# A hybrid encoder layer on one core: half of the mixer's output projection in seven products instead of eight

## The chip, the core and the metric

The kernel runs on one core of a Trainium2 chip. The metric is the device time of one execution in microseconds. The engines named below are TensorE (PE in the rows; PEld is its weight load), VectorE (DVE), ScalarE (ACT), GpSimd (POOL), which here mainly issues transfers, and SyncE (SP), whose queue issues nearly all loads. Each engine works through its own list of instructions in a fixed order, and semaphores tie them together.

## The reference, cut to what matters

```python
mixed = jnp.concatenate(
    [rms_norm(attn, g_attn_out[i]), rms_norm(rec, g_rec_out[i])], axis=-1) @ w_out[i]
h = h + rms_norm(mixed, g_mix_post[i])
fn = rms_norm(h, g_ffn_pre[i])
ff = (jax.nn.silu(fn @ w_ffn_gate[i]) * (fn @ w_ffn_up[i])) @ w_ffn_down[i]
```

There are 256 rows and 2048 columns. The output projection is the product with w_out (2048 by 2048, fp32). In front of it stand attention and a recurrent block, behind it the FFN and a per-layer embedding.

## The kernel before

**How the work is tiled.** Every large product is cut into column chunks of 512 and pairs of row blocks (two blocks of 128 rows of the weights). One *tile* is one such pair, 128 x 1024 values, 512 KB. Each tile is loaded into a raw buffer (`wr`, four of them), ScalarE casts it to fp32r (`wh`, line 661), VectorE takes the remainder of that cast (`wl`, line 677), and TensorE multiplies: for each of two row blocks and two halves of the 256 activations three products of 128 x 512, high by high, low by high, high by low (lines 715 to 717). That is 12 matmuls a tile. Four pairs of `wh` and `wl` exist, so a tile can be cast only when the tile four places ahead of it has been multiplied; a raw buffer is free again after `wl`.

**Seven products.** In the FFN, two neighbouring column chunks of one pair of row blocks are taken together as a 2 x 2 by 2 x 2 block product, in Winograd's form: seven products instead of eight, 21 matmuls instead of 24. Sums of weight blocks (lines 605 to 611, and one by a transfer that adds, line 630) and of activation blocks (`sums_of`, lines 827 to 834, and a split) are made first. Such a *unit* has four parts: `four_products` (two tiles, 12 matmuls, into all four accumulators), `made_of_four` (differences between the accumulators), `two_products` (6 matmuls) and `one_product` (3 matmuls).

**The output projection.** Chunks 0, 1 and 2 take turns, tile by tile, through eight pairs of row blocks (attention's four, `A_KS`, then the recurrent block's four, `R_KS`); chunk 3 follows alone. `sub_post` then squares each chunk and multiplies it by a gain into `mg` (lines 1558 and 1540); `next_norm` makes the root from the squares and adds `mg` times it to the residual `h` (line 1598). Two tiles of the embedding's product (`embedding`) stand between chunk 3 and the transposes of `h` (line 334), with which the FFN begins. `open_p2` opens the second stage's memory when chunk 0 ends, and `load_p2` loads the gain, `pw` and `h` from there.

**What sets the order.** A planner (`Plan`) keeps a clock for each engine while the program is written and puts into each engine's list whatever it expects to be able to start first. So a change in one place can reorder the side work on VectorE and ScalarE anywhere later. On the chip nothing is reordered.

Of the kernel before, what the change touches and what calls it, by code (L numbers as in the profile page):

```python
# [16 lines left out]
P = 128  # L17
# [10 lines left out]
N = 512  # L28
# [12 lines left out]
DOWN_KS = (0, 2, 4, 6)  # L41
PLE_KS = (0, 2)
BEGIN = (6, 7)
OUT = (3, 6, 7, 1)
# [11 lines left out]
    ),  # L56
    (lambda c: (("w_ple_gate", c), ("w_ple_gate", c + 1)), (2,), PLE_KS),
]

# [184 lines left out]
def layer(ctx: ExitStack, tc: tile.TileContext, a: dict, out: bass.AP):  # L244
# [160 lines left out]
    class Chunk:  # L405
        def __init__(self, post, before=None, late=0.0, slot="acc"):
            self.post, self.before, self.late, self.slot = post, before, late, slot
            self.accs, self.made = None, None
            self.ready, self.free = Event(), Event()
# [30 lines left out]
    class Group:  # L440
# [23 lines left out]
        def two(self, j):  # L464
            i = len(tiles)
            tiles.append(None)
            self.twos[j] = i
            lower[self.own[j] + 1] = -1
            segs.append((two_products, self, j, i))
# [70 lines left out]
    def load_stream():  # L540
        for i, tl in enumerate(tiles):
# [3 lines left out]
            w, k, n0 = tl  # L545
            if min(fours) <= i < i_ple:
                if i in lower:
                    yield (ev_spilled, ev_half_spilled, ev_unmerged)[(0, 0, 1, 2, 2)[lower[i]]]
                yield dma(ISSUE, take=raw_kind(i))
                t = lower_tile(lower[i]) if i in lower else raw_tile(i)  # L550
                nc.sync.dma_start(t, a[w][n0 // N, k // 2])
                plan.now += COST["landing"]
                if i in ev_load:
                    loaded[i] = t
                    done(ev_load[i])
                else:
                    raws[i] = t
                    done(ev_raw[i, 2])
                continue
            if i in ev_load:  # L560
# [26 lines left out]
    def sum_stream():  # L587

        for i in sorted(fours):
            at_end = i in ends_with  # L590
            for e in () if at_end else fours[i][4].values():
                yield e
# [5 lines left out]
            if at_end:  # L598
                yield ev_big
            elif n or j == 3:  # L600
                yield ev_half_spilled
            Q, R = loaded.pop(i), loaded.pop(i + 1)
            yield dve(N, take=None if at_end else f"T{n}")
            both = last_blocks(2)[:, 2 * j : 2 * j + 2, :] if at_end else blocks()[:, b0 : b + 1 : b - b0, :]
            nc.vector.tensor_tensor(out=both[:, 0, :], in0=Q[:, 0, :], in1=Q[:, 1, :], op=ALU.add)
            yield dve(N, take=None if at_end else f"t{j}")
            nc.vector.tensor_tensor(out=both[:, 1, :], in0=both[:, 0, :], in1=R[:, 1, :], op=ALU.add)  # L607
# [7 lines left out]

    ends_with, ends_in = {}, {}

    def last_blocks(i):
# [15 lines left out]
    def last_sum(i):  # L634
        late, last, j, js, _, _ = fours[i]
        b = OUT[j]
        there, at_end = Event(), i in ends_with
        yield from added(last_blocks(2)[:, 2 * j + 1, :] if at_end else blocks()[:, b, :], late[:, 0, :], there)
        yield there
        if j == js[-1]:  # L640
            raws[last] = last_blocks(2)[:, 1:4:2, :] if at_end else blocks()[:, slice(3, 7, 3) if not js[0] else slice(1, 8, 6) if js[1:] else slice(7, 8), :]
            done(ev_raw[last, 2])
# [21 lines left out]
    def ffn_fours():  # L664
        return {i: f for i, f in fours.items() if i not in ends_with}

# [72 lines left out]
    def four_products(group, j, i):  # L739
# [3 lines left out]
        first, last = j == 0, j == len(group.sevens) - 1  # L743
        if first:
            C1.open()
            C2.open()
        plan.main(0, ev_lo[i, 2], group.lhs.ev[kx], ev_s, C1.ready, C2.ready)
        s = group.lhs.sums[kx]
        product(C2.accs[0], s["S1"], i, 0, first, last)
        product(C2.accs[1], s["S2"], i, 1, first, last)  # L750
        spent(i)
        plan.main(0, ev_lo[i + 1, 2])
        product(C1.accs[0], block(group.lhs, kx, 0), i + 1, 0, first, last)
        product(C1.accs[1], s["S7"], i + 1, 1, first, last)
        spent(i + 1)
        if last:
            plan.add(made_of_four(group), plan.clk["pe"] + plan.SEM, -SOON)
            plan.run()

    def made_of_four(group):  # L760
# [49 lines left out]
    def sums_of(lhs, kx, hi, lo):  # L810
# [6 lines left out]
        yield lhs.ev[kx + 1]  # L817
        kind = "mid" if lhs is hP else "T4"
        for j in range(2):
            h, l = lhs.at[kx + j]  # L820
            yield dve(S, take=None if j else kind)
            if not j and lhs is hP:
                at_ = mid_tile()
# [541 lines left out]
    def attend(g):  # L1365
# [32 lines left out]
        yield ev_in  # L1398
        at_hi, at_lo = hT_pair("attn")
        mixT.blocks(at_hi, at_lo, 2, H - 2, 2)  # L1400
        for bs in ((2, 6), (4,)):
            plan.add(attn_norm(bs, ra, at_hi, at_lo), plan.now)

    at0 = tuple(at.tile([P, 2, S], F32R, name=f"at0_{n}") for n in ("hi", "lo"))
# [51 lines left out]
    def open_p2():  # L1456
# [4 lines left out]
        t2["pool"] = rs  # L1461
        t2["h"], t2["mg"] = Halves(rs, "h"), Halves(rs, "mg")
        t2["ple"] = rs.tile([P, NT, D], F32, name="ple")
        t2["third"] = rs.tile([P, 2, N], F32, name="third")
        plan.add(load_p2(), plan.clk["pe"])

    pT = [Act(2)] * 2
# [14 lines left out]
    def load_p2():  # L1482
# [15 lines left out]
        pT[0].blocks(hi, lo, 0, 2)  # L1498
        pT[0].pair(0)

    ev_sums_back = Event()

    class Sub:
# [10 lines left out]
        def chunk(self, c, ch, add=False):  # L1514
# [9 lines left out]
            for t in range(NT):  # L1524
                src = ch.accs[t]
                if add:
                    yield dve(N)
# [200 lines left out]
    def after_mix():  # L1728
# [3 lines left out]
    A_KS = [(k, k) for k in range(0, 8, 2)]  # L1732
    OPEN = 3
    ch = [
        Chunk(sub_post(mix, c, after=after_mix), None if c else open_p2,
              slot="sm" if c == 2 else "acc")
        for c in range(4)
    ]
# [399 lines left out]
    n = 0  # L2138
    for i in range(min(fours), max(f[1] for f in ffn_fours().values())):
# [4 lines left out]
    for i in range(min(fours), max(f[1] for f in fours.values() if f[4] is hF.ev_sums)):  # L2144
        if i % (W_BUFS + MORE_W) < MORE_W:
# [4 lines left out]
    for i, (_, last, _, js, _, two) in fours.items():  # L2150
        ev_load[i], ev_load[i + 1] = Event(), Event()
        if i in ends_with:
            gives[i], gives[i + 1], gives[two], gives[last] = "x", raw_kind(i), "x", "x"
            continue
# [21 lines left out]

    soonest = min(fours)
    plan.add(load_stream(), late=lambda: (
# [105 lines left out]
```

## Time and profile before

| | |
|---|---|
| median of 3 runs | 1148.32 us (1145.85 to 1148.58) |
| span of the profiled execution, first to last instruction | 1144.3 us |
| TensorE busy | 1134.3 us, 99% of the span |
| VectorE busy | 945.8 us, 83% |
| ScalarE busy | 732.1 us, 64% |

The profile gives the span of one execution; the times of runs also hold what lies around the span, so the median stands 4.0 us above it. Busy time of an engine says how full it is on average. Whether it sets the time is read from what TensorE waited for.

### The profile page before, as it was taken

What the parts mean: (1) busy time and instruction counts of PE and PEld (TensorE: products, weight loads), DVE (VectorE), ACT (ScalarE), POOL (GpSimd) and SP (SyncE); (2) the same over time, 40 slices, a digit from 0 to 9 for tenths busy, and PEclk for the clock granted to TensorE, in tenths of its full rate; (3) what the DMA queues carried; (4) which work ended last, traced back from release to release, by engine and by line L of the source; (5) the groups of instructions that cost most, each with busy time, mean ns of one, the idle gap of its engine ahead of it and who ended that gap; (6) DMA issues with size and microseconds to landing.
All of it is one profiled execution on the core that took longest, in us unless ns stands there. A gap on an engine that the chain in (4) does not pass through costs nothing.

```text
span 1144.3 us, 15197 instructions
## 1 busy us (share of the span) xinstructions
PE 1134.3 (99%) x5175; PEld 942.3 (82%) x5175; DVE 945.8 (83%) x1201; ACT 732.1 (64%) x967; POOL 149.3 (13%) x236
## 2 busy tenths in 40 slices
PE   9999999999999999999999999999999999999997
PEld 7888888888888888888888888888888888888886
DVE  6578697888468779899997898999988888888885
ACT  6777877876447655666566556556564565576674
POOL 0000000000000032132010133232111313100200
PEclk9999999999999999999999999999999999999999
DMA  9867666546685996887877777797797777967862
GB/s 321 288 194 218 180 193 198 167 158 204 208 313 172 300 299 214 230 249 213 279 271 219 260 223 215 249 266 243 258 314 244 229 244 227 285 242 254 257 208 95
DMA packets 110846, 269.01 MB, mean 235 GB/s; under 512 B 36336, under 2 KB 43248, under 8 KB 109360
## 3 DMA queue, kind: packets, MB, share of 16 engines
q1 hardware_dynamic: 96304, 243.17, 63.3%
q0 software_dynamic: 14032, 24.52, 11.2%
q8 instruction: 40, 0.66, 0.2%
q10 hardware_dynamic: 432, 0.35, 0.1%
q14 instruction: 38, 0.31, 0.1%
HBM read 250.17 MB, written 9.44 MB: 227 GB/s over the span
## 4 chain that ended last, share of the span: by engine, by line
PE 92%; DVE 3%; DMA 2%; ACT 2%; issue 1%; SPq 0%; DVEq 0%; ACTq 0%
PE acc L717 23%; PE acc L716 23%; PE acc L715 23%; PE acc L728 7%; PE acc L726 7%; PE acc L727 7%; DVE wl L677 1%; PE tr L334 1%; DMA mg<-part 1%; ACT wh L661 1%; DMA sq<-ev 0%; PE half L2012 0%; PE acc L2012 0%; PE pg L366 0%; PE pg L365 0%
## 5 line engine op out<-in xcount | busy, mean ns | idle before, releaser
L677 DVE TENSOR_TENSOR wl<-wr,wh 128x1024 fp32r<-128x1024 f32 (+1 forms) x300 | 358.9, 1210 | 91.6 <-ACT wh L661 90.2
L661 ACT CAST wh<-wr 128x1024 fp32r<-128x1024 f32 (+1 forms) x300 | 310.8, 1043 | 164.3 <-PE acc L716 112.1
L353 POOL DMA_DIRECT2D mT<-mid x164 | 96.1, 597 | 610.6 <-DMA lower<-in_w_ffn_up 401.1
L716 PE MATMUL acc<-wh,hT_mix_lo 128*128 128x512 f32 x420 | 163.6, 390 | 0.3 <-DVE hT_mix_lo L323 0.3
L715 PE MATMUL acc<-wh,hT_mix_hi 128*128 128x512 f32 x420 | 163.7, 390 | 0.0
L717 PE MATMUL acc<-wl,hT_mix_hi 128*128 128x512 f32 x420 | 163.4, 389 | 0.0
L717 PE MATMUL acc<-wl,hT_hi 128*128 128x512 f32 x320 | 124.5, 390 | 0.0
L715 PE MATMUL acc<-wh,hT_hi 128*128 128x512 f32 x316 | 124.4, 394 | 0.0
L716 PE MATMUL acc<-wh,hT_lo 128*128 128x512 f32 x316 | 123.1, 390 | 0.0
L661 ACT CAST wh<-ple 128x1024 fp32r<-128x1024 f32 (+1 forms) x68 | 68.2, 1008 | 77.4 <-DVE ple L607 47.7
L716 PEld LDWEIGHTS acc<-wh,hT_mix_lo 128*128 128x128 f32 x420 | 78.8, 188 | 17.1 <-DVE hT_mix_lo L323 1.0
L715 PEld LDWEIGHTS acc<-wh,hT_mix_hi 128*128 128x128 f32 x420 | 78.9, 188 | 16.3
L717 PEld LDWEIGHTS acc<-wl,hT_mix_hi 128*128 128x128 f32 x420 | 78.8, 188 | 16.4
L677 DVE TENSOR_TENSOR wl<-ple,wh 128x1024 fp32r<-128x1024 f32 (+1 forms) x68 | 79.2, 1165 | 10.1 <-ACT wh L661 9.7
L717 PEld LDWEIGHTS acc<-wl,hT_hi 128*128 128x128 f32 x320 | 60.0, 188 | 12.8
L716 PEld LDWEIGHTS acc<-wh,hT_lo 128*128 128x128 f32 x316 | 59.4, 188 | 11.6
L715 PEld LDWEIGHTS acc<-wh,hT_hi 128*128 128x128 f32 x316 | 59.4, 188 | 11.4
L630 POOL DMA_DIRECT2D ple<-in_w_ffn_up x27 | 24.1, 892 | 162.9 <-DVE wl L677 121.9
L661 ACT CAST wh<-third 128x1024 fp32r<-128x1024 f32 x33 | 34.7, 1052 | 13.9 <-PE acc L716 8.2
L677 DVE TENSOR_TENSOR wl<-third,wh 128x1024 fp32r<-128x1024 f32 x33 | 40.2, 1219 | 0.7 <-ACT wh L661 0.5
L661 ACT CAST wh<-lower 128x1024 fp32r<-128x1024 f32 x30 | 31.4, 1051 | 13.9 <-PE acc L716 12.4
L677 DVE TENSOR_TENSOR wl<-lower,wh 128x1024 fp32r<-128x1024 f32 x30 | 36.3, 1217 | 1.8 <-ACT wh L661 1.8
(463 smaller groups left out, 2481.1 us busy)
## 6 DMA issues: line engine op xcount, KB each, us to landing
wr<-in_w_in SPq DMA_DIRECT2D x77, 512.0 KB, 4.3
wr<-in_w_ffn_gate SPq DMA_DIRECT2D x73, 512.0 KB, 5.2
wr<-in_w_ffn_down SPq DMA_DIRECT2D x55, 512.0 KB, 5.6
wr<-in_w_ffn_up SPq DMA_DIRECT2D x51, 512.0 KB, 4.8
wr<-in_w_out SPq DMA_DIRECT2D x32, 512.0 KB, 4.4
wr<-in_w_ple_gate SPq DMA_DIRECT2D x30, 512.0 KB, 4.7
lower<-in_w_ffn_up SPq DMA_DIRECT2D x21, 512.0 KB, 5.9
lower<-in_w_ffn_down SPq DMA_DIRECT2D x17, 512.0 KB, 5.7
```

Of the source, the lines that this page charges most:

```text
L334: nc.tensor.transpose(tr[:, b, t * P : (t + 1) * P], e[:, t, sl], ident)
L353: (nc.gpsimd if i in pool else nc.sync).dma_start(dst[32 * j : 32 * j + 32, :, :, i, :], src[32 * i : 32 * i + 32, :, :, j, :],)
L630: nc.gpsimd.dma_start(dst, src, accum_op=ALU.add)
L661: nc.scalar.copy(his[i][:, 0 : src.shape[1], :] if n == 2 else his[i][:, j, :], src)
L677: nc.vector.tensor_tensor(out=los[i][:, m, :], in0=src, in1=f32(his[i][:, m, :]), op=ALU.subtract)
L715: nc.tensor.matmul(accs[t], hi[:, sl], his[i][:, j, :], start=st, stop=False, **group)
L716: nc.tensor.matmul(accs[t], lo[:, sl], his[i][:, j, :], start=False, stop=False, **group)
L717: nc.tensor.matmul(accs[t], hi[:, sl], los[i][:, j, :], start=False, stop=sp, **group)
L726: nc.tensor.matmul(dst, x[0], wh, start=start, stop=False, skip_group_check=seeded)
L727: nc.tensor.matmul(dst, x[1], wh, start=False, stop=False, skip_group_check=seeded)
L728: nc.tensor.matmul(dst, x[0], wl, start=False, stop=stop, skip_group_check=seeded)
```

## The change

Chunks 2 and 3 are now worked together. Their recurrent pairs (`R_KS`) stay at eight products a pair (`rest_products`), and their four attention pairs become units of seven products. Each unit's first four products go into four accumulator banks of their own (`four_accs`), shared by the four units, and `added_four` adds their sums and differences into the two chunks' accumulators. The second tile of each unit is loaded to a place of its own (`parked`), the weight sums stand in the tile `ple`, and `out_sums` makes the sums of attention blocks. The second stage's memory is opened at chunk 0's sixth tile, and `h`, which shares its memory with the parked tiles, is loaded after the units' `two` parts.

```diff
+OUT_KS = (0, 2, 4, 6)
+OUT_AT = (1, 2, 2, 3)
+OUT_OPEN = 5
...
+            if i in ev_load and i < i_out:
+                first = i in outs
+                if not first:
+                    yield ev_p2
+                yield dma(512, take=raw_kind(i) if first else None)
+                loaded[i] = raw_tile(i) if first else parked(outs[i - 1])
+                nc.sync.dma_start(loaded[i], a[w][n0 // N, k // 2])
...
+        q1, q7, q5, q6 = group.four_accs if out else (*C1.accs, *C2.accs)
...
+    def added_four(group):
+        (C1, _, _), (C2, _, _) = group.chunks
+        q1, q7, q5, q6 = group.four_accs
...
+        nc.scalar.copy(x, q1)
+        nc.vector.tensor_tensor(out=u, in0=x, in1=q6, op=ALU.subtract)
+        nc.vector.tensor_tensor(out=v, in0=u, in1=q7, op=ALU.subtract)
+        nc.vector.tensor_tensor(out=u, in0=q5, in1=u, op=ALU.subtract)
+        for n, (C, t, y) in enumerate(((C1, 0, x), (C1, 1, v), (C2, 0, u), (C2, 1, v))):
+            if n % 2 == 0:
+                yield ev_rest_of[n // 2]
+            if n == 3:
+                nc.vector.tensor_tensor(out=v, in0=q5, in1=v, op=ALU.subtract)
+            nc.vector.tensor_tensor(out=C.accs[t], in0=C.accs[t], in1=y, op=ALU.add)
+            done(ev_added[n])
...
+    def out_two(group, j, i):
...
+        plan.main(0, ev_lo[i, 2], mixT.ev[kx + 1], ev_added[0])
+        product(C1.accs[0], block(mixT, kx + 1, 0), i, 0, seeded=True)
+        plan.main(0, ev_added[2])
+        product(C2.accs[0], mixT.sums[kx]["S4"], i, 1, seeded=True)
...
+    def out_one(group, j, i):
...
+        plan.main(0, ev_lo[i, 2], ev_added[1])
+        product(C1.accs[1], block(mixT, kx + 1, 1), i, 0, seeded=True)
...
+    def out_sums():
+        yield ev_out_at
+        for i, kx in enumerate(OUT_KS):
+            yield from sums_of(
+                mixT, kx, *(x[:, 8 + 2 * i : 10 + 2 * i, :].rearrange("p k s -> p (k s)") for x in out_at)
+            )
...
         done(here)
-        for t in range(NT):
-            yield dma(1024)
-            nc.sync.dma_start(t2["h"][:, t, :], a["x"][t * P : (t + 1) * P, :])
-        done(ev_h)
         yield here
...
+        yield ev_lo[max(out_pair.twos.values()), 2]
+        t2["h"] = Halves(t2["pool"], "h")
+        for t in range(NT):
+            yield dma(1024)
+            nc.sync.dma_start(t2["h"][:, t, :], a["x"][t * P : (t + 1) * P, :])
+        done(ev_h)
...
-    three = [(ch[c], "w_out", c * N) for c in range(OPEN)]
-    turns(three, mixT, A_KS, end=False)
-    turns(three, mixT, R_KS, apart=2, begin=False)
-    for c in range(OPEN, 4):
-        seg(ch[c], "w_out", c * N, mixT, A_KS + R_KS)
+    pairs = [[(ch[c + i], "w_out", (c + i) * N) for i in range(2)] for c in (0, 2)]
+    out_pair = Group(pairs[1], mixT, A_KS + R_KS, OUT_KS)
...
+    for i, k in enumerate(A_KS + R_KS):
+        for n, (c, w, n0) in enumerate(pairs[0]):
+            seg(c, w, n0, mixT, [k], i == 0, i == 7, None if n or i != OUT_OPEN else open_p2)
+    for i, k in enumerate(R_KS):
+        for j, at_ in enumerate(OUT_AT):
+            if i == at_:
+                outs[len(tiles)] = j
+                out_pair.four(j)
+        for n, (c, w, n0) in enumerate(pairs[1]):
+            segs.append((rest_products, c, k, i, n, len(tiles)))
```

So TensorE's order becomes: sixteen tiles of chunks 0 and 1; then, with r for a rest tile (12 matmuls), Fa and Fb for the two tiles of a unit's `four` (6 each), T for a `two` (6) and O for a `one` (3): r r, F1a F1b, r r, F2a F2b, F3a F3b, r r, F4a F4b, r r, T1 to T4, O1 to O4; then the two embedding tiles and the transposes.

VectorE's list of the changed kernel, around the sums of the fourth unit (line 709 is the old 677; `wl<-ple` is F4a's remainder, the next `wl<-wr` F4b's; L932 and L321 end the sums of the fourth attention pair, which F4a multiplies with).

```order
300 L619 TENSOR_TENSOR ple<-wr 128x512
301 L621 TENSOR_TENSOR ple<-ple,parked_2926 128x512
302 L625 TENSOR_TENSOR wr<-wr,parked_2926 128x512
303 L932 TENSOR_TENSOR mid<-mid 128x128 x2
304 L709 TENSOR_TENSOR wl<-ple,wh 128x1024
305 L932 TENSOR_TENSOR mid<-mid 128x128 x2
306 L709 TENSOR_TENSOR wl<-wr,wh 128x1024
307 L321 TENSOR_TENSOR attn_lo<-mid,attn_hi 128x512
```

Before, VectorE had at chunk 3 nothing but five remainders in a row and the end of the projection behind them.

```order
265 L677 TENSOR_TENSOR wl<-wr,wh 128x1024 x3
266 L317 TENSOR_TENSOR pTl<-pw,pTh 128x512
267 L677 TENSOR_TENSOR wl<-wr,wh 128x1024 x5
268 L1540 TENSOR_TENSOR mg_2884<-acc_2975,gain_g_mix_post 128x512
269 L1540 TENSOR_TENSOR mg_2885<-acc_2976,gain_g_mix_post 128x512
```

In the changed list the low part of the fourth pair's sums comes last, behind both remainders of the unit that multiplies with it.

ScalarE's list of the changed kernel at the end of the projection: the casts of T1 to T4 (`parked`), of O1 to O3 and O4 (`wh<-ple`), of the embedding's two tiles (`wh<-wr` x2) and of the FFN's first, and the squares of chunk 3 (acc_2871, acc_2872) and chunk 2 (acc_2845, acc_2846).

```order
225 L693 CAST wh<-parked_2926 128x1024 x2
226 L693 CAST wh<-ple 128x512 x3
227 L1673 ACTIVATE junk,ss_mix<-acc_2871 128x512
228 L1673 ACTIVATE junk,ss_mix<-acc_2872 128x512
229 L1673 ACTIVATE junk,ss_mix<-acc_2845 128x512
230 L693 CAST wh<-ple 128x512
231 L693 CAST wh<-wr 128x1024 x2
232 L1673 ACTIVATE junk,ss_mix<-acc_2846 128x512
233 L693 CAST wh<-wr 128x1024
234 L375 ACTIVATE rt_mix<-tot_mix,eps 128x2
```

Before, the last casts ran ahead of the last squares:

```order
214 L661 CAST wh<-wr 128x1024 x5
215 L1558 ACTIVATE junk,ss_mix<-acc_2975 128x512
216 L1558 ACTIVATE junk,ss_mix<-acc_2976 128x512
217 L661 CAST wh<-wr 128x1024
218 L371 ACTIVATE rt_mix<-tot_mix,eps 128x2
```

Now three squares stand in front of the casts of O4 and of both embedding tiles. In SP's queue the loads of `h` moved behind the loads of the FFN's first two tiles (before, they stood among the last loads of w_out).

## Rows read from the trace of the kernel before

**Rows 1.** The page: span, and busy time of the engines.

```profile
span 1144.3 us, 15197 instructions
...
PE 1134.3 (99%) x5175; PEld 942.3 (82%) x5175; DVE 945.8 (83%) x1201; ACT 732.1 (64%) x967; POOL 149.3 (13%) x236
```

**Rows 2.** TensorE's waits, whole kernel, first and last of six: total, times, longest.

```profile
PE final L2098 <- ACT diag L2096: 2.3, 1, 2.3
...
PE acc L716 <- DVE hT_ffn_lo L323: 0.2, 1, 0.2
```

**Rows 3.** Windows: us, busy time (and instructions) by engine, granted clock, DMA share, GB/s.

```profile
285.00:300.00 15.00, 15.00 (x68) 12.43 (x67) 7.35 (x6) 6.04 (x6) 0.00 (x0) 1.00 0.68 228
350.00:360.00 10.00, 9.73 (x51) 7.67 (x50) 9.72 (x20) 7.85 (x16) 0.00 (x0) 1.00 0.62 210
1135.00:1140.00 5.00, 2.17 (x6) 0.51 (x4) 4.69 (x11) 3.18 (x6) 0.00 (x0) 1.00 0.53 208
```

**Rows 4.** TensorE's timeline, output projection to FFN: start, duration, instruction.

```profile
255.26 0.39 PE L715 MATMUL acc<-wh,at_hi 128*128 128x512 f32 x1
...
289.29 0.39 PE L715 MATMUL acc<-wh,rec_hi 128*128 128x512 f32 x1
...
300.17 0.39 PE L715 MATMUL acc<-wh,rec_hi 128*128 128x512 f32 x1
...
349.14 1.47 PE L334 MATMUL tr<-ident,h 128*128 128x128 f32 x12
350.37 0.48 PE L715 MATMUL acc<-wh,hT_mix_hi 128*128 128x512 f32 x1
...
354.01 1.03 PE L334 MATMUL tr<-ident,h 128*128 128x128 f32 x8
354.80 0.48 PE L715 MATMUL acc<-wh,hT_mix_hi 128*128 128x512 f32 x1
```

**Rows 5.** VectorE's timeline: remainders, sums of activations, sums of weights.

```profile
264.71 3.49 DVE L677 TENSOR_TENSOR wl<-wr,wh 128x1024 fp32r<-128x1024 f32 x3
...
366.55 0.42 DVE L827 TENSOR_TENSOR ple<-hT_mix_hi,hT_mix_lo 128x256 f32<-128x256 f32 x1
366.88 1.22 DVE L677 TENSOR_TENSOR wl<-wr,wh 128x1024 fp32r<-128x1024 f32 x1
...
461.00 0.69 DVE L605 TENSOR_TENSOR ple<-wr 128x512 f32<-128x512 f32 x1
461.72 0.69 DVE L607 TENSOR_TENSOR ple<-ple 128x512 f32<-128x512 f32 x1
462.33 0.68 DVE L611 TENSOR_TENSOR wr<-wr,ple 128x512 f32<-128x512 f32 x1
462.93 2.35 DVE L677 TENSOR_TENSOR wl<-wr,wh 128x1024 fp32r<-128x1024 f32 x2
...
1063.89 1.02 DVE L834 TENSOR_TENSOR mid<-mid 128x128 f32<-128x128 f32 x4
```

**Rows 6.** ScalarE's timeline: a cast in the steady state, squares of chunk 1, casts.

```profile
289.27 1.05 ACT L661 CAST wh<-wr 128x1024 fp32r<-128x1024 f32 x1 [1.67 <-PE acc L716]
...
316.07 0.60 ACT L1558 ACTIVATE junk<-acc 128x512 f32<-128x512 f32 x1 [1.27 <-PE acc L717]
...
316.75 0.60 ACT L1558 ACTIVATE junk<-acc 128x512 f32<-128x512 f32 x1
...
317.34 1.04 ACT L661 CAST wh<-wr 128x1024 fp32r<-128x1024 f32 x1
...
328.30 0.62 ACT L315 CAST pTh<-pw 128x512 fp32r<-128x512 f32 x1
```

**Rows 7.** Loads issued between 300 and 360 us: count, KB each, median us to landing.

```profile
wr<-in_w_out SPq DMA_DIRECT2D x10, 512.0 KB, 4.4
h<-in_x SPq DMA_DIRECT2D x2, 1024.0 KB, 8.0
...
wr<-in_w_ple_proj SPq DMA_DIRECT2D x2, 512.0 KB, 6.7
```

More of the change, by code (lines that the diff above doesn't have):

```diff
@@ L467, in two @@
             self.twos[j] = i
-            lower[self.own[j] + 1] = -1
+            if self.lhs is not mixT:
+                lower[self.own[j] + 1] = -1
             segs.append((two_products, self, j, i))
@@ L616, in layer, with parked, summed @@
     ends_with, ends_in = {}, {}
+    outs, ev_p2, ev_parked, ev_out_at = {}, Event(), Event(), Event()
+    def parked(j):
+        n = f"parked{j // 2}"
+        if n not in t2:
+            t2[n] = t2["pool"].tile([P, 2, 2, N], F32, tag=f"h{j // 2}", name=n)
+        return t2[n][:, j % 2, :, :]
+    def summed(j):
+        return blocks()[:, 2 * j : 2 * j + 2, :]
     def last_blocks(i):
@@ L637, in last_sum @@
         there, at_end = Event(), i in ends_with
-        yield from added(last_blocks(2)[:, 2 * j + 1, :] if at_end else blocks()[:, b, :], late[:, 0, :], there)
+        yield from added(
+            last_blocks(2)[:, 2 * j + 1, :] if at_end else summed(j)[:, 1, :] if i in outs else blocks()[:, b, :],
+            late[:, 0, :], there,
+        )
         yield there
+        if i in outs:
+            raws[last] = summed(j)[:, 1:2, :]
+            done(ev_raw[last, 2])
+            return
         if j == js[-1]:
@@ L664, in ffn_fours @@
     def ffn_fours():
-        return {i: f for i, f in fours.items() if i not in ends_with}
+        return {i: f for i, f in fours.items() if i not in ends_with and i not in outs}
     def lo_stream():
@@ L743, in four_products @@
         first, last = j == 0, j == len(group.sevens) - 1
-        if first:
+        out = group.lhs is mixT
+        if first and out:
+            ready = Event()
+            ready.t = plan.gather("acc", 2 * NT)
+            group.four_accs = [ps.tile([P, N], F32, tag="acc", name="four") for _ in range(2 * NT)]
+        elif first:
             C1.open()
             C2.open()
-        plan.main(0, ev_lo[i, 2], group.lhs.ev[kx], ev_s, C1.ready, C2.ready)
+        q1, q7, q5, q6 = group.four_accs if out else (*C1.accs, *C2.accs)
@@ L748, in four_products @@
+        plan.main(0, ev_lo[i, 2], group.lhs.ev[kx], ev_s, *((ready,) if out and first else () if out else (C1.ready, C2.ready)))
         s = group.lhs.sums[kx]
-        product(C2.accs[0], s["S1"], i, 0, first, last)
-        product(C2.accs[1], s["S2"], i, 1, first, last)
+        product(q5, s["S1"], i, 0, first, last)
+        product(q6, s["S2"], i, 1, first, last)
         spent(i)
         plan.main(0, ev_lo[i + 1, 2])
-        product(C1.accs[0], block(group.lhs, kx, 0), i + 1, 0, first, last)
@@ L821, in sums_of @@
             yield dve(S, take=None if j else kind)
-            if not j and lhs is hP:
+            if not j and lhs is not hF:
                 at_ = mid_tile()
@@ L1525, in chunk @@
                 src = ch.accs[t]
+                if t and ch.last:
+                    yield ch.last
                 if add:
```

91 lines of the change are left out of this document (72 added, 19 removed).

## The prediction

> **What bounds the kernel now.** I read the page first: TensorE is busy for 1134.3 of 1144.3 us [rows 1]. Busy matmul time can hide waiting, so I read its waits next: six in the whole kernel, 4.9 us together, the longest 2.3 us at the very end, none in the output projection [rows 2]. So TensorE sets the time nearly everywhere: a matmul less is time gained, unless one of the engines that feed it falls behind. Those engines are not idle everywhere: in 285 to 300 VectorE has 7.35 of 15 us to do, but where the FFN begins, in 350 to 360, 9.72 of 10 [rows 3].
>
> TensorE's timeline gives the unit of the sum. From 289.29 to 300.17 stand 48 matmuls: 0.2267 us each [rows 4], 2.72 us a tile of twelve. The projection begins at 255.26; the first product with the recurrent block, twelve tiles later, at 289.29, so 1.40 us beside the twelve tiles (32.63) went to a few transposes and a small product. 408 matmuls (34 tiles) and these 1.40 us end at 349.14, where the transposes of h begin: no gap.
>
> **What the change takes away.** Four units at 21 matmuls instead of 24: twelve matmuls, **-2.72 us**. Nothing else leaves TensorE. It is 0.24% of the time, less than the 0.3% that a measurement of this kernel can tell from no change. The question is what the feeding engines give back.
>
> **What VectorE gets.** Prices from start to start: a remainder 1.135 (three records end after 3.49, the last lasts 1.22), a weight sum of 512 columns 0.61 (0.72 where the next one reads its result), so 1.93 for the three of a unit, an activation sum of 256 columns 0.33, one of 128 columns 0.245 [rows 5]. Each unit adds three weight sums, and its casts and remainders cover seven row blocks instead of four; each attention pair adds two sums of 256, four of 128 and a split.
>
> I follow VectorE's list against TensorE's clock. The sixteen tiles of chunks 0 and 1 end at 255.26 + 1.40 + 16 x 2.72 = 300.17 (the order of the attention and recurrent work ahead of it is unchanged). The first row that TensorE holds up is chunk 0's product with the gain: it waits for a square that can start 0.42 before the tile's end, as chunk 1's did before (316.07, with ten tiles after 289.29 ending at 316.49 [rows 4, 6]). Chunk 0 ends at 297.45, the square starts at 297.03, the product 0.7 later at 297.74. From there to the end of the low part of the fourth pair's sums the list has 13 remainders (14.76), 16 operations of 512 columns (9.92 with the dependent ones), 4 of 256 (1.34) and 8 of 128 (1.96): 27.98 us, so it ends at 325.7 even if VectorE never waits.
>
> TensorE wants it earlier. After 300.17 stand six rest tiles and three units' F parts, 6 x 2.72 + 3 x 2.72 = 24.48: F4a begins at 324.65, and its second matmul, the first with a low sum, is due at 324.87. It waits 0.9 us, and 0.1 for semaphores. VectorE's own waits in this stretch add to that. The loads just make it: F2a's tile gets the raw buffer of the second rest tile, whose remainder ends at 301.0 by the same list, and lands 4.4 later [rows 7] at 305.5, which is when VectorE comes to it. I take **+1.0 us**, between 0.5 (prices a little high) and 2.0 (one load at the longest landing).
>
> Earlier rows keep slack: by the same count every remainder up to F4b ends 0.8 to 2.7 us before the third matmul of its tile.
>
> **The tail.** Call B the end of the last rest tile. The adds into the accumulators need the last F part and the rest tiles; by the list they end at 0.5 (first of chunk 3), in time for T1's second product at B + 0.68. T1 to T4 end at 5.44, O1 to O4 would at 8.16, the embedding at 13.60. But ScalarE has three squares in front of O4's cast, and the first reads the accumulator that T4 completes: it starts at 5.70. Squares follow each other after 0.68 and a cast follows one after 0.59 [rows 6]: O4's cast starts at 7.65, the first embedding tile's at 8.15 (casts of 512 and 1024 last 0.62 and 1.05, overlapping by 0.1), ends at 9.20, its remainder lasts 1.22 and ends at 10.45. TensorE's third matmul of that tile needs it and was due at 8.16 + 0.45 = 8.61. So the tail loses **+1.9 us**: 0.4 at O3 (its remainder stands behind the product with the gain that waits for the first square), 0.6 at O4, 0.9 at the first embedding tile. Before, this was covered: casts ran about three tiles ahead, held up only by TensorE (a cast waits 1.67 for PE [rows 6]). The bounds are 1.2 (if the first square can start as early as T4's first product allows) and 2.4 (if O2's or O3's cast is late too).
>
> **The start of the FFN.** The embedding now ends at B + 15.5. The root needs the last square, and h's first two sums end at about 15.05, so the transposes just begin on time. The second h load is issued when T4's remainder is done, at 4.0; with the 8.0 us that h took before [rows 7] it is there at 12.0, h's sum comes at 14.3: no wait. The list now puts four transposes before the first six products instead of twelve before twelve. Before, the first product came 1.23 after the transposes' start and 12 transposes and 12 products took 4.87 (349.14 to 354.01 [rows 4]). Now the first low part waits for two more sums of h and a remainder (two times 0.4 and 1.135) and comes at 2.05; six products end at 3.2, eight transposes (0.79) and six products at 5.35: **+0.5 us**, between 0 and 2.0 (the rival on the FFN's loads).
>
> **Rest of the kernel.** The planner reorders FFN side work, but TensorE's products there are the same in number, and before it waited in the whole FFN only fractions of a microsecond [rows 2]. I take 0, from -0.5 (the small waits vanish) to +2 (ten new waits of 0.2).
>
> The parked loads move no more bytes (the same 32 tiles; one block of each unit is read once more by the adding transfers, 1 MB in all). The DMA share is 0.68 in 285 to 300 [rows 3], and SP issues ten loads more without waiting for long.
>
> **Sum.** -2.72 + 1.0 + 1.9 + 0.5 = +0.7 us, against the profiled execution's span of 1144.3, so 1145.0. What lies around the span (4.0 us to the median) is unchanged: **1149.0 us**. The single terms' bounds would give -1.5 to +5.7.
>
> A rule speaks against the change in another way. TensorE's granted clock stayed at 1.00 (the 2.4 GHz level) in the stretch with its longest wait, 2.3 us behind a dense stream [rows 2, 3]. The Trainium skill (TensorE: Matmul & The Clock Gate, HAM oscillation) says that gaps between bursts of matmuls let the clock fall to half, and that matmuls behind each gap then run slow. By the row the sum stays at +0.7; by the rule, if it held for gaps of 1 us, the embedding and the first FFN tile behind the tail's gaps would run at half rate, which is the third rival below. The trace so far agrees with the row: that one long wait cost no clock in its window.
>
> **The rivals.**
> *The gain stands* (0.15). The feeding engines keep up: VectorE starts its list earlier, or the waits in the tail are taken by buffers already filled. For it speaks that TensorE has hardly a wait in 900 us of the same seven-product scheme in the FFN; against it that there casts and remainders run alongside one unit at a time, while here VectorE has 28 us of work in the 27 us up to F4a. Time: 1148.32 - 2.7 = 1145.6.
> *VectorE's debt is carried into the FFN* (0.11; the other side). TensorE reaches the transposes with VectorE about 1.4 us behind where it stood before (two sums of h done ahead of the transposes instead of seven, at 0.4, less the head start), in a stretch where VectorE has 0.28 us free in 10 [rows 3]. If the loads of the FFN's third and fourth tiles come late as well, the debt turns into waits: the third tile's load is issued only after the embedding's first remainder (10.5); landing after 4.4 us it is in time, after 6.7, as two loads did beside h [rows 7], its cast holds up the first transposed block behind it in ScalarE's list, +2.1 us. Then two or three following tiles wait for remainders, 0.5 to 1 us each: 1149.0 + 2.1 + 2.0 = 1153.1. It decides for slower when the landing takes over about 7 us, or VectorE is 3 us behind.
> *The clock falls* (0.02). Some 36 matmuls behind the gaps at half rate, at 0.2267 more each: +8, 1157.
>
> **How the numbers follow.** My forecast, a tie with some 0.7 us lost (1147 to 1151), has 0.72, the gain 0.15, the debt 0.11, the clock 0.02. The predicted time is the likeliest one's, 1149.0. Between its own range and the rivals, 1146.2 to 1152.0 leaves out the upper half of the debt and the lower part of the gain, together under 2 in 10. The 0.3% reach from 1144.9 to 1151.8. The gain of 2.7 us lies within them, and only scatter (the three runs spread over 2.7 us) brings it below: faster 0.05. Slower takes the debt and the clock: 0.12. Same: 0.83.
>
> **What would show it.** Right: twelve PE matmuls fewer; a wait of about 1 us at F4a for the low sums; waits at O3, O4 and the first embedding tile for `wh` and `wl`, 1.9 together; the transposes about 0.2 us later than 349.14; no wait over 0.5 in the FFN. Wrong: no wait at F4a or in the tail (the gain stands); a wait for a load in the stage or for h; waits that go on behind 360 us; a granted clock under 1.00 behind a gap.

## The result, and the profile after

The changed kernel takes 1152.36 us (median of 5 runs, 1151.77 to 1154.73), before 1148.32 in the same session (5 runs, 1145.85 to 1148.74). The comparison over all runs of both gives 1.0050 times as long, 95% interval 1.0039 to 1.0061. The two medians alone would give 1.0035: the one of before fell high here; in the four later sessions, with 15 to 35 runs each, it was 1146.76 to 1146.98. So the change is slower by half a per cent, and the time lies 0.36 us beyond the upper end of the range.

Page of the changed kernel; the row of engines answers to [rows 1]:

```profile
span 1150.7 us, 15270 instructions
...
PE 1136.3 (99%) x5163; PEld 940.1 (82%) x5163; DVE 972.6 (85%) x1257; ACT 738.9 (64%) x978; POOL 152.8 (13%) x240
```

Twelve matmuls fewer (the units take in eight of the projection's 32 tiles, so a quarter of it, where the title says half), and yet TensorE is busy 2 us longer: matmuls overlap, and those behind a wait last longer (0.50 for 0.39 in the timeline below), so busy time hides a part of the waiting. Its waits (total, times, longest) say more; none of these stood in [rows 2]:

```profile
PE acc L758 <- ACT wh L693: 1.6, 2, 1.1
PE acc L749 <- DVE wl L709: 1.2, 2, 0.9
...
PE acc L760 <- DVE wl L709: 1.0, 2, 0.5
PE four L758 <- ACT attn_hi L319: 0.8, 1, 0.8
PE four L759 <- DVE attn_lo L321: 0.5, 1, 0.5
```

To see where the time went, I cut both timelines at the same matmuls: the second last of the projection's sixteenth tile (the 1441st matmul, at 299.72 in before), the first transpose of `h`, the first product with `sf`, the first with `mid2h` (third down projection), the next transposes of `h`, the first `final`. Each stage is a difference of two starts, in us. All kernels of the study are in it; "e13" is the changed kernel profiled again.

| kernel | output projection | FFN start | FFN middle | third down proj. | emb. gate | time / before (95%) |
|---|---|---|---|---|---|---|
| before | 49.42 | 76.97 | 546.04 | 72.85 | 90.03 | |
| changed | 51.27 | 77.38 | 546.04 | 75.94 | 91.09 | 1.0050 (1.0039, 1.0061) |
| e13, changed again | 51.55 | 77.28 | 546.04 | 76.29 | 89.89 | 1.0045 (1.0033, 1.0058) |
| e1 phase | 51.61 | 77.28 | 546.04 | 73.79 | 90.03 | 1.0026 (1.0015, 1.0037) |
| e2 phase back | 49.42 | 76.98 | 546.04 | 74.85 | 89.93 | 1.0022 (1.0014, 1.0031) |
| e3 sums | 57.95 | 77.31 | 546.04 | 73.12 | 89.89 | 1.0051 (1.0034, 1.0068) |
| e4 tail | 55.59 | 79.30 | 546.64 | 72.14 | 89.90 | 1.0069 (1.0056, 1.0082) |
| e5 last cast | 51.75 | 77.31 | 546.04 | 73.26 | 89.90 | 1.0018 (1.0009, 1.0026) |
| e6 last sums | 50.27 | 77.31 | 546.04 | 74.16 | 89.88 | 1.0012 (1.0003, 1.0021) |
| e7 squares split | 50.56 | 77.70 | 546.04 | 72.45 | 89.88 | 1.0008 (0.9999, 1.0017) |
| e8 twelve less | 46.70 | 76.98 | 546.04 | 73.71 | 90.04 | 0.9975 (0.9966, 0.9984) |
| e9 three pairs | 49.32 | 77.76 | 546.04 | 72.69 | 89.90 | 1.0001 (0.9992, 1.0010) |
| e10 three, cast | 47.70 | 78.01 | 546.04 | 72.88 | 90.07 | 0.9995 (0.9986, 1.0003) |
| e11 phase one | 49.42 | 76.97 | 546.04 | 72.38 | 90.02 | 1.0004 (0.9996, 1.0013) |
| e12 phase two | 49.42 | 76.98 | 546.04 | 73.47 | 90.00 | 1.0002 (0.9993, 1.0010) |
| e14, e10 again | 48.00 | 78.03 | 546.05 | 74.31 | 89.90 | 0.9995 (0.9986, 1.0004) |

The reader sees two losses far apart: 1.85 us in the output projection, where 2.72 should have been won, and 3.09 in the third down projection, 620 us after the last changed line. Between them the start of the FFN takes 0.41 us more, and its middle is the same to a hundredth. The 1.06 us in the embedding gate did not come again in e13, so it belongs to that execution (VectorE waited 0.64 us there for a load into `ends`).

The output projection. TensorE's timeline of the changed kernel, start, duration, instruction, and in brackets the wait:

```profile
324.85 0.39 PE L749 MATMUL acc<-wl,rec_hi 128*128 128x512 f32 x1
325.99 0.50 PE L758 MATMUL four<-wh,attn_hi 128*128 128x512 f32 x1 [0.75 <-ACT attn_hi L319]
326.98 0.50 PE L759 MATMUL four<-wh,attn_lo 128*128 128x512 f32 x1 [0.48 <-DVE attn_lo L321]
...
342.40 0.39 PE L760 MATMUL acc<-wl,attn_hi 128*128 128x512 f32 x1
343.91 0.50 PE L758 MATMUL acc<-wh,attn_hi 128*128 128x512 f32 x1 [1.13 <-ACT wh L693]
344.25 0.40 PE L759 MATMUL acc<-wh,attn_lo 128*128 128x512 f32 x1
344.64 0.50 PE L760 MATMUL acc<-wl,attn_hi 128*128 128x512 f32 x1
...
346.12 0.50 PE L749 MATMUL acc<-wl,pTh 128*128 128x512 f32 x1 [0.32 <-DVE wl L709]
```

Read starts, not brackets: from 324.85 to 325.99 are 1.14 us where 0.2267 is the plain distance, so this wait costs 0.91, not 0.75, and the distance after a wait is 0.34 again. Added up over the stage, the eleven distances above 0.3 us hold 4.36 us beyond the plain ones, small ones 0.20: -2.72 + 4.56 = +1.84. At F4a (both waits and the distance behind them) it is 1.78, in the tail (from 342.40) 2.47.

VectorE's and ScalarE's rows of the changed kernel beside it:

```profile
312.79 0.69 DVE L621 TENSOR_TENSOR ple<-ple,parked 128x512 f32<-128x512 f32 x1 [0.65 <-DMA parked<-in_w_out]
...
323.56 1.23 DVE L709 TENSOR_TENSOR wl<-ple,wh 128x1024 fp32r<-128x1024 f32 x1
324.70 0.48 DVE L932 TENSOR_TENSOR mid<-mid 128x128 f32<-128x128 f32 x2
...
326.24 0.68 DVE L321 TENSOR_TENSOR attn_lo<-mid,attn_hi 128x512 fp32r<-128x512 f32 x1
...
340.79 0.69 DVE L1655 TENSOR_TENSOR mg<-acc,gain_g_mix_post 128x512 f32<-128x512 f32 x1 [0.50 <-PE acc L760]
...
973.83 0.69 DVE L321 TENSOR_TENSOR mid2l<-mT,mid2h 128x512 fp32r<-128x512 f32 x1 [1.66 <-ACT mid2h L319]
974.44 1.22 DVE L709 TENSOR_TENSOR wl<-wr,wh 128x1024 fp32r<-128x1024 f32 x1
975.57 0.68 DVE L321 TENSOR_TENSOR mid2l<-mT,mid2h 128x512 fp32r<-128x512 f32 x1
976.18 1.22 DVE L709 TENSOR_TENSOR wl<-ple,wh 128x1024 fp32r<-128x1024 f32 x1
```

```profile
325.33 0.61 ACT L319 CAST attn_hi<-mid 128x512 fp32r<-128x512 f32 x1
...
339.20 0.62 ACT L693 CAST wh<-ple 128x512 fp32r<-128x512 f32 x1 [0.73 <-PE acc L759]
341.51 0.60 ACT L1673 ACTIVATE junk<-acc 128x512 f32<-128x512 f32 x1 [1.69 <-DVE mg L1655]
...
342.67 0.60 ACT L1673 ACTIVATE junk<-acc 128x512 f32<-128x512 f32 x1
...
343.24 0.62 ACT L693 CAST wh<-ple 128x512 fp32r<-128x512 f32 x1
343.75 1.06 ACT L693 CAST wh<-wr 128x1024 fp32r<-128x1024 f32 x1
```

The low sums end at 326.92, 1.2 later than my list. The first product of F4a waits for `attn_hi`, which ScalarE casts at 325.33, right behind the last sum (it ends at 325.18 on VectorE). That wait adds nothing of its own: the second product was due at 325.31 and needs the low sums of 326.92 in any case. In the tail the first square waits for the product with the gain, not the other way round as I had it, so O4's cast starts at 343.24, four microseconds after O3's, with ScalarE idle for 1.69 of them.

The third down projection. The last four rows of VectorE above belong to it. The same place in before:

```profile
969.17 1.23 DVE L677 TENSOR_TENSOR wl<-ple,wh 128x1024 fp32r<-128x1024 f32 x1 [1.15 <-ACT wh L661]
970.32 1.29 DVE L317 TENSOR_TENSOR mid2l<-mT,mid2h 128x512 fp32r<-128x512 f32 x2
971.90 1.23 DVE L677 TENSOR_TENSOR wl<-third,wh 128x1024 fp32r<-128x1024 f32 x1 [0.29 <-ACT wh L661]
```

Before, a remainder that TensorE needs goes first, and the low part of `mid2`, which comes late through a transposing transfer, behind it. In the changed kernel the low part stands in front of two remainders and holds them up while VectorE idles 1.66 us for it. TensorE then waits for the first of the two:

```profile
975.71 0.50 PE L760 MATMUL acc<-wl,mid2h 128*128 128x512 f32 x1 [0.43 <-DVE wl L709]
```

### The profile page after: what moved, and what is told of

Read it like the earlier page. It is cut to its first block, busy times and chain, and to the rows that moved or that the text cites. A ratio compares the mean times of both kernels' runs of the same rounds, so it can differ in the third digit from the quotient of the medians.

```text
span 1150.7 us, 15270 instructions
## 1 busy us (share of the span) xinstructions
PE 1136.3 (99%) x5163; PEld 940.1 (82%) x5163; DVE 972.6 (85%) x1257; ACT 738.9 (64%) x978; POOL 152.8 (13%) x240
## 4 chain that ended last, share of the span: by engine, by line
PE 85%; DVE 6%; DMA 5%; ACT 2%; issue 1%; POOL 0%; SPq 0%; DVEq 0%; ACTq 0%; POOLq 0%
PE acc L749 20%; PE acc L747 20%; PE acc L748 20%; PE acc L760 6%; PE acc L758 6%; PE acc L759 6%; DVE wl L709 2%; DMA mT<-mid 2%; PE tr L338 1%; ACT wh L693 1%; DMA ends<-in_w_ple_gate 1%; DMA pw<-in_pT 1%; DMA parked<-in_w_out 1%; DMA sq<-ev 0%; PE warm L2327 0%
## 5 line engine op out<-in xcount | busy, mean ns | idle before, releaser
L709 DVE TENSOR_TENSOR wl<-wr,wh 128x1024 fp32r<-128x1024 f32 (+1 forms) x293 | 350.4, 1208 | 65.5 <-ACT wh L693 61.4
L693 ACT CAST wh<-wr 128x1024 fp32r<-128x1024 f32 (+1 forms) x293 | 302.7, 1042 | 142.3 <-PE acc L748 87.7
L747 PE MATMUL acc<-wh,hT_mix_hi 128*128 128x512 f32 x408 | 159.1, 390 | 0.6 <-ACT hT_mix_hi L325 0.6
L748 PE MATMUL acc<-wh,hT_mix_lo 128*128 128x512 f32 x408 | 158.8, 389 | 0.0
L749 PE MATMUL acc<-wl,hT_mix_hi 128*128 128x512 f32 x408 | 158.8, 389 | 0.0
L693 ACT CAST wh<-ple 128x1024 fp32r<-128x1024 f32 (+1 forms) x78 | 76.5, 986 | 77.0 <-DVE ple L621 43.4
L709 DVE TENSOR_TENSOR wl<-ple,wh 128x1024 fp32r<-128x1024 f32 (+1 forms) x78 | 88.5, 1137 | 9.0 <-ACT wh L693 8.4
L655 POOL DMA_DIRECT2D ple<-in_w_out x4 | 3.6, 890 | 320.6 <-DMA wr<-in_w_out 302.8
L693 ACT CAST w<-wr 128x1024 fp32r<-128x1024 f32 x29 | 30.6, 1054 | 16.8 <-PE acc L748 13.7
```

Of the source, the lines that this page charges most:

```text
L655: nc.gpsimd.dma_start(dst, src, accum_op=ALU.add)
L693: nc.scalar.copy(his[i][:, 0 : src.shape[1], :] if n == 2 else his[i][:, j, :], src)
L709: nc.vector.tensor_tensor(out=los[i][:, m, :], in0=src, in1=f32(his[i][:, m, :]), op=ALU.subtract)
L747: nc.tensor.matmul(accs[t], hi[:, sl], his[i][:, j, :], start=st, stop=False, **group)
L748: nc.tensor.matmul(accs[t], lo[:, sl], his[i][:, j, :], start=False, stop=False, **group)
L749: nc.tensor.matmul(accs[t], hi[:, sl], los[i][:, j, :], start=False, stop=sp, **group)
```

## The experiments

My theory for the far loss: the planner. The changed projection has eight entries more in its list of tiles (40 for 32), and which FFN tiles get the fifth pair of weight buffers is decided by the tile's number modulo five. Rival: the FFN loses because it begins 2.5 us late against its loads.

**e1 and e2, the numbering alone.** e1 is the changed kernel with

```diff
-        if i % (W_BUFS + MORE_W) < MORE_W:
-            more_w[i] = i % (W_BUFS + MORE_W)
+        if (i - 8) % (W_BUFS + MORE_W) < MORE_W:
+            more_w[i] = (i - 8) % (W_BUFS + MORE_W)
```

and e2 is the kernel before with `(i + 8)` there. On TensorE, VectorE and ScalarE e1 then has the list of the changed kernel up to the start of the FFN and that of before from there on, and e2 the reverse.

> The changed kernel with one number different: the tiles that take the fifth pair of weight buffers are counted from eight tiles later, so that the same tiles of the feed-forward part take it as in the kernel before. The output projection is that of the change; the feed-forward part has the order of instructions of the kernel before. Theory (the shift by eight tiles turns the order of the feed-forward part, and the third down projection then waits for remainders): the offset against before stays at +2.5 us from 428 us on instead of growing by 3.1 in the third down projection and by 1.1 in the embedding gate, so 1152.4 - 4.2 = 1148.2 us. Rival (the feed-forward part loses because it starts 2.5 us late against its loads, in whatever order): 1152.4 us, with the same waits at 975 to 1006 us.

> The kernel before with one number different: the fifth pair of weight buffers goes to the tiles that the changed kernel gives it to. The output projection is that of before; the feed-forward part has the order of the changed kernel. Theory (the order alone costs it): 1148.3 + 4.2 = 1152.5 us, with waits of TensorE for remainders in the third down projection though it starts no later. Rival (the late start): no change, 1148.3 us.

Measured: e1 1150.41 us (before beside it 1146.98), e2 1149.31. The two halves add up: 0.26% and 0.22% against 0.50% and 0.45% for both. The theory holds, with 2 to 2.5 us in place of 4.2: in e2, whose FFN starts no later than before's, the third down projection takes 2.00 longer, and VectorE stands at the same row:

```profile
970.42 0.69 DVE L317 TENSOR_TENSOR mid2l<-mT,mid2h 128x512 fp32r<-128x512 f32 x1 [2.40 <-ACT mid2h L315]
971.03 1.22 DVE L677 TENSOR_TENSOR wl<-wr,wh 128x1024 fp32r<-128x1024 f32 x1
```

e1 starts 3 us late and gets back all but 0.9. Eleven profiles have before's order in that stage (all but the changed kernel, e13, e2, e11 and e12); it takes 72.14 to 74.31 us there, and 74.85 to 76.29 in the three of the changed order.

The starts of TensorE's products say which part of this the order brings. In the first 20 us of the stage nothing beyond the plain distances is lost in those eleven nor in e11 and e12, and 1.20, 1.52 and 1.69 us are lost in e2, the changed kernel and e13. In the next 20 us it is 1.56, 2.34 and 2.52 there, but 0.05 to 2.22 elsewhere, with 0.79 in e10 and 2.22 in e14, which are one kernel. So the order costs 1.2 to 1.7 us in these 20 us in every profile that has it; how much of the later waits it brings can't be told from their scatter.

**e11 and e12, other numberings of before,** `(i + 1)` and `(i + 2)` in the same line.

> The kernel before with the fifth pair of weight buffers given to the tiles one earlier (another order of the feed-forward part that was not that of either kernel). Theory (before's order is one of several, and each meets the crowded third down projection in its own way): the stretch from the first product of the third down projection to the next transposes, 72.85 us in before and 74.85 in e2, comes out anywhere between 72 and 77 us, with the whole moving by as much. Rival (only the shift of the changed kernel is bad, by a collision of its own): 72.9 us, no change in time.

> As e11, with the pair given to the tiles two earlier. Theory: again its own value between 72 and 77 us for that stretch. Rival: 72.9 us, no change.

Measured 72.38 and 73.47, times 1.0004 and 1.0002. This one goes to the rival: of the four numberings tried, only the changed kernel's is bad.

**e3, the sums of the attention pairs earlier** (on e1):

```diff
-        plan.add(out_sums(), plan.clk["pe"], 0.5)
+        plan.add(out_sums(), plan.clk["pe"], -0.5)
```

> e1 with the sums of the attention row blocks taken earlier among VectorE's work (their lateness -0.5 in place of 0.5), so that the last pair's sums, the low ones too, are done before the last four weight sums. Theory (the first product of the fourth pair waits because the low sums stand behind two casts on VectorE): the waits of 0.75 and 0.48 us there and the slow matmuls behind them go, 1.2 to 2.0 us, so 1146.2 to 1147.0 us when e1 is at 1148.2. Rival (VectorE is full there, so that the casts moved behind are late in their turn): the wait stands at another tile of the same stage and the time is that of e1.

The theory fell: the wait at F4a went, but the products with the gain of chunks 0 and 1 moved back, and these free the four banks that F1a needs. Waits, then windows of e3 (us, engines, granted clock, DMA):

```profile
PE four L758 <- DVE mg L1655: 2.4, 1, 2.4
```

```profile
306.00:310.00 4.00, 1.57 (x8) 0.98 (x6) 3.65 (x7) 1.41 (x2) 0.00 (x0) 1.00 0.69 152
310.00:313.00 3.00, 2.32 (x7) 1.40 (x8) 3.00 (x4) 1.05 (x1) 0.00 (x0) 0.66 0.00 0
313.00:318.00 5.00, 5.00 (x14) 3.90 (x13) 4.51 (x6) 1.04 (x1) 0.85 (x1) 0.52 1.01 315
```

The clock fell to its lower level (1.2 of 2.4 GHz) behind the gap: 14 matmuls in 5 us. It fell once more in the tail of this profile. There the distances are those of the changed kernel (1.51 us at O4, 0.75 at the embedding), and yet the clock behind them was 0.53 here (first line) and 1.00 in the changed kernel (second line):

```profile
352.00:355.50 3.50, 3.50 (x9) 2.79 (x10) 3.50 (x7) 2.50 (x6) 0.00 (x0) 0.53 0.64 179
347.00:351.00 4.00, 4.00 (x19) 3.30 (x18) 4.00 (x10) 2.96 (x6) 0.00 (x0) 1.00 0.84 268
```

The six executions lie between 1150.1 and 1156.1 us; the profile shows one of the two longest.

**e4, squares and products with the gain later** (on e1), and **e5**, the same with 0.6 for 1.0:

```diff
-                plan.add(self.squares(c, t, src, squared[t]), plan.now)
+                plan.add(self.squares(c, t, src, squared[t]), plan.now, ch.late)
...
-        Chunk(sub_post(mix, c, after=after_mix), slot="sm" if c > 1 else "acc") for c in range(4)
+        Chunk(sub_post(mix, c, after=after_mix), late=1.0 if c > 1 else 0.0, slot="sm" if c > 1 else "acc") for c in range(4)
```

> e1 with the squares and the products with the gain of column chunks 2 and 3 planned later by 1, so that ScalarE casts the last seventh-product tile and the two first embedding tiles ahead of the squares. Theory (ScalarE's squares in front of the casts cost the tail): the waits of 1.13 and 0.32 us at the last product and the first embedding tile go, with the slow matmuls behind them 1.5 to 2.1 us, so 1146.1 to 1146.7 us when e1 is at 1148.2. Rival (the norm of the sum, which the same squares feed, ends later by as much, and the transposes wait for it): 1148.2 us or more, with the wait in front of the first transposes.

> e1 with the squares and gain products of chunks 2 and 3 planned later by 0.6 in place of 1 (e4): on ScalarE only the cast of the last seventh-product tile goes ahead of the three squares, the embedding's casts stay behind them. Theory (ScalarE is the engine that ends last in the tail): the wait of 1.13 us at the last product goes, but the casts of the embedding end when they did, so that the wait of 0.32 us there grows to about 1.5 us: no change against e1, 3.0 us above before. Rival (the place of the one cast is all that cost): 1.1 to 1.5 us faster than e1.

In e4 the waits of the tail went, and one wait for the root of the norm came, as the rival said; behind it the clock was 0.50 from 356 to 361:

```profile
355.17 2.10 PE L338 MATMUL tr<-ident,h 128*128 128x128 f32 x8 [5.36 <-ACT rt_mix L375]
```

In e5 the wait at O4 went and came back one tile on, and the stage is the same within 0.14 us. The theory holds, that ScalarE's list as a whole ends last there and not one cast alone:

```profile
344.59 0.50 PE L747 MATMUL acc<-wh,pTh 128*128 128x512 f32 x1 [0.87 <-ACT wh L693]
...
345.85 0.50 PE L749 MATMUL acc<-wl,pTh 128*128 128x512 f32 x1 [0.53 <-DVE wl L709]
```

**e6, the last pair's sums alone earlier** (on e5); **e7**, e6 with 0.8 for 0.6, which sets casts and squares alternately:

```diff
-        plan.add(out_sums(), plan.clk["pe"], 0.5)
+        plan.add(out_sums(), plan.clk["pe"], late=lambda: -1.0 if at_sum[0] == 3 else 0.5)
```

> e5, and the sums of the last attention pair alone are taken earlier (lateness -1 from the fourth pair on, 0.5 for the three others as in the change): the low sums then stand ahead of the last remainder cast but one, the others stay where they are, unlike in e3. Theory (the wait at the fourth pair's first products is this one row's place on VectorE): the waits of 0.7 and 0.5 us and the slow matmuls behind them go, 1.2 to 2.0 us less than e5 at the last seven-product group. Rival (VectorE has no room there: what goes ahead makes another row late): a wait of the same size at the remainder of another tile within 320 to 332 us, and the time of e5.

> e6 with the squares and gain products planned later by 0.8: on ScalarE the order is last cast, square, embedding cast, square, embedding cast, so that neither the embedding nor the norm is put off as a whole. Theory: it gains the 1.5 to 2 us of the tail that e4 gained there, without e4's wait of 5.4 us for the norm, 2.5 to 3.5 us less than e1 in all with e6's part, that is the time of before within 1 us. Rival (squares are needed as early as they stood in e1): a wait for the norm at the first transposes of 1 us or more, and no gain over e6.

e6 gains 1.48 in the stage, as expected (by time 0.8, and the intervals of e5 and e6 overlap); a distance of 0.65 is left at F4a, and two of 0.41 and 0.47 come among the T parts. e7's tail is 1.1 better still (one distance of 0.93, for 1.26 and 0.92), but in its profile the second unit's loads came late, which costs it 1.4 more there than e6, with the same lists at that place. VectorE of e7:

```profile
312.51 0.69 DVE L619 TENSOR_TENSOR ple<-wr 128x512 f32<-128x512 f32 x1 [1.32 <-DMA wr<-in_w_out]
313.82 0.69 DVE L621 TENSOR_TENSOR ple<-ple,parked 128x512 f32<-128x512 f32 x1 [0.62 <-DMA parked<-in_w_out]
```

By time e7 can't be told from before (1.0008, interval from 0.9999): the theory of the tail holds, without a gain over before.

**e8, the price of twelve matmuls.** Before, with the matmuls of one tile skipped (`if i in skip: continue`), its load, cast and remainder kept.

> The kernel before without the twelve matmuls of one w_out tile (one row-block pair of chunk 3 is left out of the sum), everything else in its order. It prices what the change removes. Theory: 12 x 0.2267 = 2.72 us less at the first transposes, and at the end, 0.24% below before. Rival (the remainders or the feed-forward part's loads end last and take it back): the offset of -2.7 us shrinks by the end to -1 us or less.

The result of this kernel lacks that tile's product; it serves for the time alone. The stage shrinks by 2.72 us to the hundredth, the time by 0.25% (0.16 to 0.34). The rival falls: what is won there stays won, but for 0.9 in the third down projection, within that stage's spread.

**e9, three units instead of four** (on e1: `OUT_KS = (0, 2, 4)`, the fourth attention pair among `rest_products`), **e10**, e9 with the squares 0.6 later as in e5, and **e14**, e10 again.

> e1 with three row-block pairs as units of seven products in place of four; the fourth attention pair goes in as plain products, in the loop with the recurrence blocks (nine matmuls fewer than before in place of twelve). Theory (VectorE has no room for the sums, and each set of seven costs the path more in waits than its three matmuls give): -9 x 0.2267 = -2.04 us, and the waits at the fourth group (1.68 us above the plain distance) and at the last cast (1.3 us) are gone, while those of the embedding's first tile (0.5 us) and the first groups stay: 0.5 to 1.5 us below before in the output projection up to the first transposes, where e1 is 2.2 us above. Rival (the same debt comes due wherever the last group stands): a wait of a microsecond or more at the third group, and the output projection ends 1 us or more above before.

> e9 with the squares and gain products of chunks 2 and 3 planned later by 0.6: ScalarE casts the first embedding tile ahead of the squares. Theory: the wait at the embedding's first tile (0.5 to 1 us) goes, and the norm, with two squares put off by one cast of 1.05 us, still ends before the transposes: 0.5 to 1 us below e9, so 1 to 2 us below before. Rival (as in e4, the norm is late by the cast): no gain over e9, with a wait at the first transposes.

> e10 once more, to narrow its interval. Theory (1.72 us less in the output projection, 1.04 us more at the first transposes, nothing else): 0.3 to 1.0 us below before, a ratio of 0.9991 to 0.9997. Rival (its median was luck): a ratio of 1.0000 or above.

In e9 no distance above 0.3 us is left ahead of the embedding, which waits 1.9 in sum; the stage ends 0.10 below before, short of the 0.5 expected. e10 takes the embedding's wait away: 47.70, 1.72 below before, with 0.29 us of waits in the whole stage. But then the first products of the FFN wait, since ScalarE copies embedding results ahead of the first `hT_mix_hi`:

```profile
348.62 0.51 PE L747 MATMUL acc<-wh,hT_mix_hi 128*128 128x512 f32 x1 [0.56 <-ACT hT_mix_hi L325]
349.43 0.50 PE L748 MATMUL acc<-wh,hT_mix_lo 128*128 128x512 f32 x1 [0.31 <-DVE hT_mix_lo L327]
```

It costs 1.04 of the 1.72; in e14 1.06 of 1.42. e10 and e14 both stand at 0.9995, both intervals reach past 1: a version that is not slower, and not shown to be faster.

**e13, the changed kernel again.**

> The changed kernel as it is, once more. Theory (the change costs 1.85 us in the output projection, 0.4 at the start of the feed-forward part and 2 in the third down projection, and the rest of its profile was that one execution): 74.5 to 75.5 us from the first product of the third down projection to the transposes, 89.9 to 90.1 us from there to the last transposes, 4.0 to 5.0 us above before. Rival (the start that is late against the loads adds its own in the feed-forward part's end): again about 76 and 91 us, 5.5 us above before.

The embedding gate is back at 89.89, so its 1.06 was chance. The third down projection is not: 76.29. e2 with the same order lost 1.4 less in its one profile, which is of the fastest of its eleven executions (1147.42, median 1149.31). Whether the late start adds to it is open; scatter of that size is there without it, since e10 and e14 differ by 1.43 in this stage.

## Why the prediction was wrong

- **What the change takes away, -2.72:** right; e8 measures it, 2.72 in the stage.
- **What VectorE gets, +1.0 at F4a:** the wait was where I put it and for the low sums, as I said, but mis-sized: 1.78, inside the bounds of 0.5 to 2.0. VectorE's list began 0.4 late, lost 0.65 to a wait for a parked load and ended 1.2 late. e6 shows that the place of these sums in the list is what costs.
- **The tail, +1.9:** mis-sized, 2.47, just above the bound of 2.4: nothing at O3 (0.4 foreseen), 1.56 at O4 (0.6 foreseen), 0.91 at the embedding (0.9 foreseen). The order of square and product [rows 6] was the other way round after the change. That ScalarE's list decides it was right (e5, e7).
- **The start of the FFN, +0.5:** right, 0.31 and 0.41.
- **Rest of the kernel, "I take 0":** this is the step that failed. I argued from the number of products and from the small waits of before, and gave -0.5 to +2; it took +3.1 and +3.4. The late start alone (e1) left 0.9 of it, within the stage's scatter. The larger part came from a number: eight list entries more turn the planner's order in the whole FFN (e1, e2), and a late row then stands in front of two remainders that TensorE waits for.
- **What lies around the span, 4.0:** wrong. It is 1.8 us in each run with its own span (1152.54 to 1150.7). The profiled execution of before was one of about 1146.1 us, 2.2 below the median I added it to. In spans the miss is 1150.7 against 1145.0; the error of the base hid 2 us of it in the times.
- **The rivals:** the debt carried into the FFN gave a time close to the measured one, 1153.1, but by luck: its mechanism did not occur, since from 360 us to the waits of the third down projection (975.71) TensorE's products never start more than 0.24 us apart. The gain stands only if the feeding work is cut: with three units 1.72 (e10) and 1.42 (e14) of 2.04 us arrive in the stage, and 1.0 of it is lost again at the start of the FFN. The clock kept 0.998 in both profiles of the changed kernel, whose longest gap ahead of the last two products is 1.5 us, but the same gaps cost it in e3, and the slowest of the five executions, 1154.73 us, has 0.995 where the others have 0.997 and 0.998; whether its clock fell in the tail is not shown, no trace of it is kept. The row that I set against this rival, the 2.3 us wait at the end of before, could not speak: only two matmuls follow that wait. The Trainium skill (TensorE: Matmul & The Clock Gate, HAM oscillation) says that gaps between bursts of matmuls let the clock drop to half. e3 (0.52 and 0.53) and e4 (0.50) agree; the changed kernel's two profiles have such gaps without a drop.

## What to carry to other kernels

When lists are made by a planner, an edit that shifts a counter is a second change, everywhere behind it; compare the lists there, and measure the shift alone on the old kernel. A saving on the full engine is worth its matmuls in the stage where they stood (e8), and each set of sums on the engines that feed it costs what it displaces: without the fourth unit (e9 against e1) the stage is 2.29 us shorter, though it has three matmuls more. Take the time around the span from a run with its own span, never from the median.

## What was not expected of the hardware

- ScalarE's square and VectorE's product read the same accumulator and do not overlap: the product runs from 340.79 for 0.69, the square begins at 341.51. For the next accumulator it is the other way round: the product at 342.81 waits 0.73 for a square. So which of the two comes first in the lists decides who waits. The Trainium skill (PSUM — Partial Sum Buffer, PSUM bank collisions raise a hardware error) says that the compiler's scheduler adds a dependency between two engines that touch the same bank and the same 32 partitions, reads and writes alike. The rows agree in that the two never overlap; what put the wait there is not shown here.
- A wait costs more than its bracket: the distance behind it is 0.34 us in place of 0.2267, once. The 0.39 and 0.45 in the tail are waits without a bracket: TensorE's weight load stood 0.43 us for `wl` there (at 344.64) and 0.24 for `wh` (at 345.06).
- Distances of 2.83 and 1.28 us close together (e3) were followed by matmuls 0.43 us apart for 5 us. Distances of 1.51 and 0.75 us close together were followed by the same for some 2.6 us in e3, and by none in the changed kernel, e13 and e1. So equal gaps did not always cost the clock; what decides is not shown.
- Ahead of the changed code, with the same instructions, the 1441st matmul started between 298.80 and 300.72 us in the sixteen profiles. Differences of a microsecond between single profiles are read by stages.
